# Feed-forward entry of a hybrid attention block: low parts and differences of two operand sets (H22, T4) made by VectorE instead of GpSimd

## The chip, the cores and the metric

The kernel runs on one core of a Trainium2 chip. A core has five engines, each with its own instruction queue: TensorE (matmul; PE in the profile, PEld its weight loads), VectorE (DVE), ScalarE (ACT), GpSimd (POOL) and SyncE (SP), which here only issues transfers. The metric is the device time of one execution in microseconds; the time of a kernel is the median over its runs.

## The reference

One transformer block over 1024 tokens of width 1024 in float32: a mixer (dilated attention and a gated delta rule side by side, with an output projection), then a gated feed-forward network of inner width 2816, then a last norm. What the change touches is the entry of the feed-forward network:

```python
h = _rmsnorm(x, norm_ffn_g[l]) * (1.0 + sc2) + sh2
y = (jax.nn.silu(h @ w_gate[l]) * (h @ w_up[l])) @ w_down[l]
x = x + g2 * y
return _rmsnorm(x, final_norm_g)
```

## The kernel before

Every large product is made in three matmuls: each float32 operand is split into a high part (a cast by ScalarE to the matmul's own format) and a low part (operand minus high part), and high by high, high by low and low by high are added up in PSUM. A low part is one subtraction of 128 x 512 elements, `h2_split` for the activations (line 1473) and `parts` for the weights (line 1580).

The products `h @ w_gate` and `h @ w_up` are made by a fast scheme that takes seven half-size products in place of eight. `h` is kept transposed as two halves of the width (four tiles of 128 each: k = 0 to 3 and 4 to 7) by two halves of the tokens (0 and 1). In `x2[d, hf]`, d is the tile of the width and hf the half of the tokens. The seven activation operands are H11 and H21 (the first half of the tokens), H22 (the second half's upper tiles), and T1 to T4, sums and differences of the quarters. Each operand consists of four tiles with a high and a low part: `H22h0`, `H22l0` and so on. The weights come as slabs of 128 x 512, 11 pairs f of gate (`wg`) and up (`wu`); their names in the profile are `wr` (as loaded), `wh` and `wl` (parts), `s` (sums).

`up_first` makes the two products that need only H11 and H21. The other five, in `rest_begin` and `up_rest`, follow one another on TensorE in the order T2, T1, T3, H22, T4, 12 matmuls each (`up_mm`, line 1590), into the PSUM banks a and c in turn. For the first three pairs f the products with H11 and H21 are made ahead (`early`), while the second half of the tokens is normed; then, from the line `t2 = []` on, VectorE and ScalarE make the five remaining operand sets:

- `normed2` (lines 1503 and 1506) norms a tile in place, VectorE and ScalarE after each other;
- T1 and T2 are differences of normed quarters (line 1596), split with low parts on VectorE;
- T3 likewise;
- H22 is the normed upper quarter itself: only a split;
- T4 is `x2[4 + k, 0] - t2[k]`, in place, then a split.

In the kernel before, the four low parts of H22, the four differences of T4 and the first two low parts of T4 are GpSimd's: ten operations. All high parts are ScalarE's.

The program is written as a list of operations with dependences; a scheduler puts each engine's operations in one fixed order, by priority and by its own estimate of when an operand is ready. Operations under `urgent()` (weight loads and parts, the sums between products) go ahead of others. So moving an operation to another engine changes the order on that engine, and of what depends on it on others. Each engine then takes its list strictly in order, waiting on semaphores.

Memory: the tiles `x2` and `t2` lie in the pool `px`, closed at `sx.close()`; the pool `po2` behind it takes the same room. It holds the raw slabs `wr2` of the second-half products, so the first of these loads wait until VectorE has read the last T3 operands.

Of the kernel before, what the change touches and what calls it, by code (L numbers as in the profile page):

```python
# [82 lines left out]
def build(tc, I, out):  # L83
    nc = tc.nc
# [442 lines left out]
    def scratch(name, n, shape):  # L527
        return [dr.tile(shape, F32, name=f"{name}{i}_d") for i in range(n)]

    class _:  # L530
# [12 lines left out]
        x2 = scratch("x2", 2, [4, P, D])  # L543
# [105 lines left out]
    t1, t2 = t12[:, 0:64], t12[:, 64:P]  # L649
# [810 lines left out]
    x2 = {}  # L1460
# [9 lines left out]
    def h2_split(name, k, src, lo_eng, copy=None):  # L1470
        hi, lo = HB[name][k]
        (copy or nc.scalar.copy)(hi, src)
        lo_eng.tensor_tensor(out=lo, in0=src, in1=hi.bitcast(F32), op=ALU.subtract)
# [121 lines left out]
    def sub(out, a, b, eng=None):  # L1595
        (eng or nc.vector).tensor_tensor(out=out, in0=a, in1=b, op=ALU.subtract)
# [133 lines left out]
    t2 = []  # L1730
# [13 lines left out]
        sub(x2[k, 1], x2[4 + k, 1], x2[k, 1])  # L1744
        h2_split("T3", k, x2[k, 1], nc.vector)
    for k in range(4):
        h2_split("H22", k, x2[4 + k, 1], nc.gpsimd)
    for k in range(4):
        sub(x2[4 + k, 0], x2[4 + k, 0], t2[k], nc.gpsimd)
        h2_split("T4", k, x2[4 + k, 0], nc.gpsimd if k < 2 else nc.vector)  # L1750
    sx.close()
    po2, so2 = pool("po2")
    for f in range(NF):
# [214 lines left out]
```

## Time and profile before

| | |
|---|---|
| median of 3 runs | 1414.42 us (1414.08, 1414.42, 1420.56) |
| the profiled execution | 1418.03 us, of it 1416.1 from the first to the last instruction |
| TensorE busy | 1354.1 us, 96% of the span |
| VectorE busy | 879.7 us, 62% |
| ScalarE busy | 661.3 us, 47% |
| GpSimd busy | 302.6 us, 21%, the last at 805.7 us |
| mean granted TensorE clock | 0.987 |

Times in the views count from the first instruction of the span. A busy share is a mean over stages; the stage of this change lies between 774 and 827 us. A row of a timeline gives the start, the duration, the engine, the line, the operation with the tiles that it writes and reads, and in brackets the time that the engine idled before it and what ended that. Rows of one line and form that follow each other are merged (x2).

### The profile page before, as it was taken

What the parts mean: (1) busy time and instruction counts of PE and PEld (TensorE: products, weight loads), DVE (VectorE), ACT (ScalarE), POOL (GpSimd) and SP (SyncE); (2) the same over time, 40 slices, a digit from 0 to 9 for tenths busy, and PEclk for the clock granted to TensorE, in tenths of its full rate; (3) what the DMA queues carried; (4) which work ended last, traced back from release to release, by engine and by line L of the source; (5) the groups of instructions that cost most, each with busy time, mean ns of one, the idle gap of its engine ahead of it and who ended that gap; (6) DMA issues with size and microseconds to landing.
All of it is one profiled execution on the core that took longest, in us unless ns stands there. A gap on an engine that the chain in (4) does not pass through costs nothing.

```text
span 1416.1 us, 24467 instructions
## 1 busy us (share of the span) xinstructions
PE 1354.1 (96%) x8984; PEld 1114.2 (79%) x8984; DVE 879.7 (62%) x1659; ACT 661.3 (47%) x1287; POOL 302.6 (21%) x277
## 2 busy tenths in 40 slices
PE   8998999999989899999999999999999999999997
PEld 5678877888888777768777778888888888888885
DVE  3688484655826433666228986757575776474487
ACT  4398424365234355766147633333333333444456
POOL 2345412443213344543252400000000000000000
PEclk9999999998999999999999999999999999999999
DMA  8656664485342345621584264545363565766566
GB/s 306 233 182 166 172 207 158 141 265 159 120 131 68 127 127 170 175 96 54 174 262 151 67 200 153 183 135 200 110 218 112 194 210 188 262 219 198 194 222 232
DMA packets 169872, 245.68 MB, mean 173 GB/s; under 512 B 32566, under 2 KB 73831, under 8 KB 169752
## 3 DMA queue, kind: packets, MB, share of 16 engines
q1 hardware_dynamic: 169752, 244.12, 53.3%
q8 instruction: 71, 1.16, 0.3%
q14 instruction: 49, 0.40, 0.1%
HBM read 181.30 MB, written 67.48 MB: 176 GB/s over the span
## 4 chain that ended last, share of the span: by engine, by line
PE 54%; DVE 5%; DMA 3%; issue 2%; ACT 1%; POOL 0%; SPq 0%; DVEq 0%; ACTq 0%; POOLq 0%
PE wua L1590 8%; PE wga L1590 8%; PE X L1785 6%; PE wuc L1590 4%; PE Z L1785 4%; PE wgc L1590 4%; PE wo L590 4%; PE g_a L590 3%; PE y L1348 2%; PE Y L1785 2%; PE tr L1331 2%; PE wgb L1590 2%; PE wub L1590 2%; PE S L1307 1%; PE S L1308 1%
## 5 line engine op out<-in xcount | busy, mean ns | idle before, releaser
L1580 DVE TENSOR_TENSOR wl_db<-wr_db,wh_db 128x512 fp32r<-128x512 f32 x77 | 53.2, 691 | 76.2 <-ACT wh_db L1579 76.0
L1579 ACT CAST wh_db<-wr_db 128x512 fp32r<-128x512 f32 x77 | 47.9, 622 | 98.0 <-PE X L1785 41.3
L1311 DVE CUSTOM_DVE_ANT_0 X<-S,ng 128x512 f32<-128x512 f32 (+3 forms) x64 | 36.8, 587 | 55.8 <-PE S L1308 38.0
L1785 PE MATMUL X<-wl_db,wh_da 128*128 128x512 f32 x176 | 68.6, 390 | 0.2 <-DVE wl_db L1580 0.2
L1785 PE MATMUL X<-wh_db,wl_da 128*128 128x512 f32 x176 | 68.5, 389 | 0.0
L1785 PE MATMUL X<-wh_db,wh_da 128*128 128x512 f32 x176 | 68.5, 389 | 0.0
L1316 ACT ACTIVATE X<-X,sc 128x128 f32<-128x128 f32 (+7 forms) x64 | 49.4, 773 | 38.5 <-DVE sc L1311 35.0
L1318 POOL TENSOR_SCALAR X<-X,sc 128x128 f32<-128x128 f32 (+7 forms) x64 | 50.5, 792 | 76.0 <-DVE sc L1317 72.6
L1580 DVE TENSOR_TENSOR wl_da<-wr_da,wh_da 128x512 fp32r<-128x512 f32 x77 | 52.7, 686 | 1.2 <-ACT wh_da L1579 1.2
L590 PE MATMUL g_a<-hh,wh_a 128*128 128x512 f32 x128 | 53.4, 417 | 0.0
L590 PE MATMUL wo<-yh,wh_wo 128*128 128x512 f32 x128 | 51.5, 405 | 0.9 <-DVE xo L1399 0.9
L590 PE MATMUL wo<-yl,wh_wo 128*128 128x512 f32 x128 | 50.4, 394 | 1.3 <-DVE yl L1410 1.3
L590 PE MATMUL g_a<-hh,wl_a 128*128 128x512 f32 x128 | 51.5, 402 | 0.0
L590 PE MATMUL g_a<-hl,wh_a 128*128 128x512 f32 x128 | 51.4, 402 | 0.0
L590 PE MATMUL wo<-yh,wl_wo 128*128 128x512 f32 x128 | 51.0, 398 | 0.0
L1579 ACT CAST wh_da<-wr_da 128x512 fp32r<-128x512 f32 x77 | 47.3, 616 | 5.9 <-PE wua L1590 5.8
L1331 PE MATMUL tr<-ident,X 128*128 128x128 f32 x288 | 44.0, 277 | 3.6 <-DVE et L1334 1.5
L1579 ACT CAST wh_wg_s<-wg_s 128x512 fp32r<-128x512 f32 x33 | 20.5, 621 | 55.1 <-PE wuc L1590 23.8
L231 POOL TENSOR_TENSOR wl_wo<-wr_wo,wh_wo 128x512 fp32r<-128x512 f32 x24 | 32.9, 1374 | 62.2 <-ACT wh_wo L230 62.2
L1331 PEld LDWEIGHTS tr<-ident,X 128*128 128x128 f32 x288 | 33.2, 140 | 13.3 <-issue 5.7
L613 PE MATMUL g_va<-wh_va,hh 128*128 128x256 f32 x128 | 38.3, 299 | 5.4 <-ACT sp_a L1096 5.4
L1348 PE MATMUL y<-et,va 128*64 128x128 f32 x576 | 43.2, 280 | 0.3 <-DVE yl L1360 0.3
(545 smaller groups left out, 4337.5 us busy)
## 6 DMA issues: line engine op xcount, KB each, us to landing
wm<-in_wada SPq DMA_DIRECT2D x44, 512.0 KB, 6.1
wr_da<-ao_d SPq DMA_DIRECT2D x77, 256.0 KB, 3.1
wr_wu<-in_wu SPq DMA_DIRECT2D x50, 256.0 KB, 2.7
wr_wg<-in_wg SPq DMA_DIRECT2D x48, 256.0 KB, 3.2
ao_d<-a SPq DMA_DIRECT2D x44, 256.0 KB, 2.4
wr_wd<-in_wdn SPq DMA_DIRECT2D x44, 256.0 KB, 3.1
wr_db<-wt_d SPq DMA_DIRECT2D x44, 256.0 KB, 2.7
ao_d<-as SPq DMA_DIRECT2D x33, 256.0 KB, 2.3
```

Source lines behind the costliest of these rows:

```text
L231: (eng or nc.gpsimd).tensor_tensor(out=lo[:, :n], in0=raw[:, :n], in1=hi[:, :n].bitcast(F32), op=ALU.subtract)
L590: last[0] = nc.tensor.matmul(ps, a[:, w0], b[k0 + k4][:, cs], start=(i == 0), stop=(i == n - 1))
L613: last[0] = nc.tensor.matmul(ps[:, :n], a[k][:, ts_], b[:, w0], start=(i == 0), stop=(i == 23))
L1311: nc.vector.tensor_tensor_reduce(out=X[:, c0:c1], in0=ps[:, 0 : c1 - c0], in1=ng[:, u + c0 : u + c1], scale=1.0, scalar=(3e38 if m is None ...
L1316: nc.scalar.activation(X[:, 0:nk], X[:, 0:nk], AF.Exp, scale=-1.0, bias=m, accum_out=sc[:, 2:3])
L1318: nc.gpsimd.tensor_scalar(out=X[:, 0:nk], in0=X[:, 0:nk], scalar1=sc[:, 3:4], scalar2=0.0, op0=ALU.mult, op1=ALU.add)
L1331: nc.tensor.transpose(ps[:, (kb - c0) * P : (kb - c0 + 1) * P], X[:, kb * P : kb * P + P], ident)
L1348: nc.tensor.matmul(yps[64 * e : 64 * e + 64, yc], va[:, kb, 64 * e : 64 * e + 64], ets[e][:, kb, :], start=(kb == 0), stop=(kb == qb),)
L1579: nc.scalar.copy(hi, src)
L1580: (eng or nc.vector).tensor_tensor(out=lo, in0=src, in1=hi.bitcast(F32), op=ALU.subtract)
L1590: nc.tensor.matmul(ps, a[:, w0], b, start=(first and k == 0 and n_ == 0), stop=(k == 3 and n_ == 2), skip_group_check=True,)
L1785: nc.tensor.matmul(bank[b], a[:, ts_], w, start=(first and f == 0 and n_ == 0), stop=(f == NF - 1 and n_ == 2), skip_group_check=True,)
```

## The change

The low parts of H22 and T4 and the differences of T4 are all given to VectorE.

```diff
@@ -1744,10 +1744,10 @@
     for k in range(4):
-        h2_split("H22", k, x2[4 + k, 1], nc.gpsimd)
+        h2_split("H22", k, x2[4 + k, 1], nc.vector)
     for k in range(4):
-        sub(x2[4 + k, 0], x2[4 + k, 0], t2[k], nc.gpsimd)
-        h2_split("T4", k, x2[4 + k, 0], nc.gpsimd if k < 2 else nc.vector)
+        sub(x2[4 + k, 0], x2[4 + k, 0], t2[k])
+        h2_split("T4", k, x2[4 + k, 0], nc.vector)
     sx.close()
```

The order of TensorE's operations and of SyncE's transfers stays as it is. On VectorE, at the end of the entry stage, between the last difference of T3 and the first product of gate and up (a11), rows come in (`x2_4_0` and its like are tiles of the first half of the tokens, names as in `x2[4, 0]`):

```order
 L1596 TENSOR_TENSOR x2_3_1_8146<-x2_7_1_8150,x2_3_1_8146 128x512
+L1473 TENSOR_TENSOR H22l0_8719<-x2_4_1_8147,H22h0_8718 128x512
+L1473 TENSOR_TENSOR H22l1_8721<-x2_5_1_8148,H22h1_8720 128x512
+L1473 TENSOR_TENSOR T3l3_8749<-x2_3_1_8146,T3h3_8748 128x512
+L1473 TENSOR_TENSOR H22l2_8723<-x2_6_1_8149,H22h2_8722 128x512
+L1473 TENSOR_TENSOR H22l3_8725<-x2_7_1_8150,H22h3_8724 128x512
+L1596 TENSOR_TENSOR x2_4_0_8151<-x2_4_0_8151,t2_0_9039 128x512
+L1596 TENSOR_TENSOR x2_5_0_8152<-x2_5_0_8152,t2_1_9048 128x512
+L1596 TENSOR_TENSOR x2_6_0_8153<-x2_6_0_8153,t2_2_9057 128x512
+L1473 TENSOR_TENSOR T4l0_8751<-x2_4_0_8151,T4h0_8750 128x512
```

All ten operations of GpSimd come in here, behind the differences of T3; nothing ahead of the T1 parts moves. The piece goes on, up to the sums of the first up-slab (`wu0_s1`):

```order
+L1599 TENSOR_TENSOR wg0_u5_9149<-wga0_8758,wg0_u5_9149 128x512
+L1473 TENSOR_TENSOR T4l1_8753<-x2_5_0_8152,T4h1_8752 128x512
 L1473 TENSOR_TENSOR T4l2_8755<-x2_6_0_8153,T4h2_8754 128x512
+L1596 TENSOR_TENSOR x2_7_0_8154<-x2_7_0_8154,t2_3_9066 128x512
+L1599 TENSOR_TENSOR wg0_u2_9148<-wgc0_9078,wg0_u2_9148 128x512
 L1473 TENSOR_TENSOR T4l3_8757<-x2_7_0_8154,T4h3_8756 128x512
-L1473 TENSOR_TENSOR T3l3_8749<-x2_3_1_8146,T3h3_8748 128x512
 L1684 TENSOR_TENSOR a11_0_9207<-p1_wg0_8772,p1_wu0_8838 128x512
 L1599 TENSOR_TENSOR wu0_s1_9221<-wr2_wu0_20_9217,wr2_wu0_21_9219 128x512
-L1599 TENSOR_TENSOR wg0_u5_9149<-wga0_8758,wg0_u5_9149 128x512
 L1596 TENSOR_TENSOR wu0_s2_9222<-wu0_s1_9221,wr_wu0_10_9213 128x512
```

The two sums of gate (`wg0_u5`, `wg0_u2`), which stood behind `wu0_s1`, now stand ahead of a11, among the T4 operations. On ScalarE the four high parts of T4 move from before the T3 parts to behind them:

```order
 L1472 CAST T3h3_8748<-x2_3_1_8146 128x512
 L1648 COPY wg0_u5_9149<-wgc0_9078 128x512
+L1472 CAST T4h0_8750<-x2_4_0_8151 128x512
+L1472 CAST T4h1_8752<-x2_5_0_8152 128x512
+L1472 CAST T4h2_8754<-x2_6_0_8153 128x512
 L1669 ACTIVATE wg0_u5_9149<-wg0_u5_9149 128x512
+L1472 CAST T4h3_8756<-x2_7_0_8154 128x512
+L1669 ACTIVATE wg0_u2_9148<-wg0_u2_9148 128x512
+L1669 ACTIVATE g21_0_9203<-wga0_8758 128x512
 L1579 CAST wh_wu0_s2_9227<-wu0_s2_9222 128x512
```

The two silu operations and g21 (line 1669), which stood among the parts of the up-slab, now stand ahead of its first high part.

## The prediction

> **What bounds the kernel now.** I looked first at the busy time by stretch (columns: stretch and length, then busy time and count of TensorE, its weight loads, VectorE, ScalarE and GpSimd, the granted clock, the DMA share, GB/s), cut where GpSimd does the ten operations that the diff moves.
>
> ```profile
> 774.00:802.20 28.20, 28.20 (x130) 23.44 (x129) 28.15 (x34) 22.10 (x40) 12.74 (x8) 1.00 0.36 112
> 802.20:827.05 24.85, 19.73 (x74) 14.27 (x74) 22.31 (x34) 10.69 (x20) 3.48 (x3) 0.93 0.36 118
> 827.05:1373.00 545.95, 545.95 (x2410) 452.09 (x2409) 360.96 (x566) 220.47 (x391) 0.00 (x0) 1.00 0.56 187
> ```
>
> Before 802.2 and from 827.05 to 1373 TensorE has no gap. Only the middle stretch can be shortened, and what is won there is kept, since TensorE alone sets the next 546 us. The timeline of TensorE shows the holes there (start, duration, operation, and in brackets the idle time and who ended it).
>
> ```profile
> 802.26 0.39 PE L1590 MATMUL wga<-T2h,wh_wg_s 128*128 128x512 f32 x1
> ...
> 806.89 0.50 PE L1590 MATMUL wga<-T2l,wh_wg_s 128*128 128x512 f32 x1 [2.20 <-DVE T2l L1473]
> ...
> 813.36 0.50 PE L1590 MATMUL wga<-T3h,wh_wg_s 128*128 128x512 f32 x1 [0.66 <-ACT wg_u L1646]
> ...
> 817.12 0.51 PE L1590 MATMUL wga<-T3l,wh_wg_s 128*128 128x512 f32 x1 [0.65 <-DVE T3l L1473]
> ...
> 824.65 0.50 PE L1590 MATMUL wua<-T2h,wl_wu_s 128*128 128x512 f32 x1 [0.88 <-DVE wl_wu_s L1580]
> ...
> 827.05 0.39 PE L1590 MATMUL wuc<-T1h,wh_wu_s 128*128 128x512 f32 x1
> ```
>
> Between the first and the last of these rows stand six blocks of 12 matmuls (wg with T2, T1, T3, H22, T4, then wu with T2). A block without a hole takes 2.72 us, as the chain of waits has it:
>
> ```profile
> 829.93 2.72 PE wua L1590 x12
> 832.65 2.72 PE wuc L1590 x12
> ```
>
> So 6 x 2.72 = 16.32 us of work took 827.05 - 802.26 = 24.79: **8.47 us are lost**, and that is the most that any change here can give. Most holes end on VectorE. VectorE itself never rests from 774 to 817, but its operations are not all of one length:
>
> ```profile
> 781.10 0.68 DVE L1599 TENSOR_TENSOR p_wu<-wub,p_wu 128x512 f32<-128x512 f32 x1
> 781.70 1.42 DVE L1580 TENSOR_TENSOR wl_wg<-wr_wg,wh_wg 128x512 fp32r<-128x512 f32 x1
> ...
> 792.47 1.79 DVE L1596 TENSOR_TENSOR wr_wg<-wr_wg,wr_wg 128x512 f32<-128x512 f32 x1
> 794.18 1.77 DVE L1473 TENSOR_TENSOR T2l<-t,T2h 128x512 fp32r<-128x512 f32 x1
> 795.88 1.77 DVE L1596 TENSOR_TENSOR x<-x,x 128x512 f32<-128x512 f32 x1
> ...
> 801.08 3.48 DVE L1473 TENSOR_TENSOR T1l<-x,T1h 128x512 fp32r<-128x512 f32 x2
> ...
> 806.15 0.68 DVE L1473 TENSOR_TENSOR T2l<-t,T2h 128x512 fp32r<-128x512 f32 x1
> ...
> 816.99 0.68 DVE L1684 TENSOR_TENSOR a<-p_wg,p_wu 128x512 f32<-128x512 f32 x1
> ```
>
> From 806.15 to 816.99 stand 18 operations: 10.84 / 18 = 0.602 us from start to start. From 781.70 to 816.99 stand 42, which at 0.602 would be 25.3 us and took 35.3: 10.0 us too much, all of it before 806.15 and in single operations that take 1.77 (0.68 elsewhere). Their places are those of GpSimd:
>
> ```profile
> 781.26 1.31 POOL L1596 TENSOR_TENSOR x<-x,t 128x512 f32<-128x512 f32 x1 [16.23 <-DVE t L1596]
> 786.20 3.38 POOL L1596 TENSOR_TENSOR x<-x,t 128x512 f32<-128x512 f32 x2 [3.63 <-DVE t L1596]
> 792.35 4.76 POOL L1473 TENSOR_TENSOR H22l<-x,H22h 128x512 fp32r<-128x512 f32 x3 [2.76 <-ACT H22h L1472]
> 798.90 1.70 POOL L1473 TENSOR_TENSOR H22l<-x,H22h 128x512 fp32r<-128x512 f32 x1 [1.80 <-ACT H22h L1472]
> 800.57 1.74 POOL L1596 TENSOR_TENSOR x<-x,t 128x512 f32<-128x512 f32 x1
> 802.28 3.41 POOL L1473 TENSOR_TENSOR T4l<-x,T4h 128x512 fp32r<-128x512 f32 x2
> ```
>
> Ten GpSimd operations, ten extra microseconds on VectorE: the two take turns, 1.70 us a pair (794.18, 795.88), about 1.1 of it GpSimd's.
>
> **The change part by part.** *Removed*: ten GpSimd operations, and with them the 10.0 us that VectorE stands behind them. *Added*: ten VectorE operations of the form in the rows above, 10 x 0.602 = 6.0 us, so VectorE as a whole is 4.0 us better off. But the order matters more than the sum: the ten stand behind the last T3 difference, so all before them (T2, T1, T3, the parts of wg's slabs) comes up to 10 us earlier, and only what follows pays the 6.0.
>
> I walk this along the new order, counting operations from the one at 781.70, at 0.602 each, plus 0.68 to the end, plus 0.4 for short waits on ScalarE: T2l0 is now reached at 782.30 and its high part is ready at 782.34 by the row below, a wait that did not show before; I allow a few of these. TensorE's demand is 802.26 plus 2.72 a block.
>
> ```profile
> 781.72 0.62 ACT L1472 CAST T2h<-t 128x512 fp32r<-128x512 f32 x1
> ```
>
> T2l3 (22 operations on): ready 796.0, wanted 804.5. T3l3 (41 on): 807.5, wanted 810.0. H22l3 (43 on): 808.7, wanted 812.7. T4l0 (47 on): 811.1, wanted 813.4. All in time, so the first holes close. T4l3 is later than its 53 places say: its high part waits for the last difference x_7_0 (51 on, ready 813.5) and ScalarE's 0.62, so it starts at 814.25 and is ready at 814.9, wanted at 815.4: 0.5 us of slack. Behind it on VectorE's queue stand a11, then the sums of the first up-slab, wu0_s1 (start 815.45) and wu0_s2, which needs wu0_s1's end (816.15 to 816.85). ScalarE's high part of wu0_s2 takes 0.62, so TensorE's wu block on T2 starts at 817.55 in place of 815.86: **1.7 us late**. Its third matmul needs the low part, three places after wu0_s2: 817.96 + 0.68 = 818.65, which costs **another 0.7**. That is the new wait; nothing else is late, and the next block starts at 818.58 + 2.4 = 820.98 in place of 827.05. Gain: 8.47 - 2.4 = **6.1 us**.
>
> What of the transfers? The up-slab's second pair of loads is released by VectorE's reads of T3l, and one of these loads is in the chain now:
>
> ```profile
> 816.46 0.61 DVE T3l L1473
> ...
> 817.09 0.33 SPq L1571
> ...
> 817.46 5.21 DMA wr_wg<-in_wg
> ...
> 822.70 0.69 DVE wg_s L1599
> ```
>
> These 5.2 us cost VectorE 2 us before wu0_s2's low part. With T3l3 ready at 807.5 even a 5.2 us load lands at 813, and its reader wg1_s1 comes at 817.4: covered by the ten inserted operations. Without that cover it would again cost 2.0. After 827 VectorE has slack: the low part of the next gate slab is made 8.6 us before its block.
>
> ```profile
> 829.33 0.68 DVE L1580 TENSOR_TENSOR wl_wg_s<-wg_s,wh_wg_s 128x512 fp32r<-128x512 f32 x1
> ...
> 837.93 0.39 PE L1590 MATMUL wga<-T2h,wh_wg_s 128*128 128x512 f32 x1
> ```
>
> In the new order it stands 67 places after 781.70 (822.8 with all waits named), wanted at 831.9: the same slack. GpSimd has no other work after this stage, so its idleness is free. ScalarE's casts of T4 move behind T3's; they are in the walk.
>
> The one price that no row gives exactly is that of the waits I put in by hand. Lower end: none (no 0.4, no wait before T4l3), then 1.4 us are lost instead of 2.4; upper end: each of the ten added operations waits 0.2 us on ScalarE (a third of its 0.62), 2 us more. I take 2.4, as the nearest rows (781.72) show waits under 0.4.
>
> The profiled execution took 1418.03 us (span 1416.1 and 1.9 around it): 1418.03 - 6.1 = 1411.9. It is 3.6 above the median of the runs, 1414.42; the stage is the same length in both as far as is known, so 1414.42 - 6.1 = **1408.3 us**.
>
> **A rule weighed.** TensorE's clock falls to half after the present hole:
>
> ```profile
> 805.47:808.88 3.41, 1.52 (x5) 0.97 (x6) 3.41 (x6) 0.81 (x2) 0.21 (x1) 1.00 0.00 0
> 808.88:812.29 3.41, 3.41 (x10) 2.62 (x8) 3.41 (x7) 2.64 (x6) 0.00 (x0) 0.50 0.23 77
> 733.79:737.20 3.41, 1.70 (x11) 1.15 (x9) 2.29 (x3) 2.28 (x5) 2.42 (x2) 1.00 0.97 267
> 737.20:740.61 3.41, 3.41 (x20) 2.82 (x19) 0.54 (x2) 1.10 (x2) 0.00 (x0) 1.00 1.04 305
> ```
>
> A window with 1.52 us of matmul was followed by 3.41 us at half clock, one with 1.70 was not. The new waits leave 3.41 - 2.4 = 1.0 us of matmul in the worst-placed 3.41 us, so a fall is possible: half of 3.41 is 1.7 us, 1410.0.
>
> The Trainium skill ("TensorE: Matmul & The Clock Gate", "What's actually happening") puts the fall after at least one idle window of about 3.4 us; by it the new waits cost no clock and the sum stays 1408.3. The trace differs: here a window that was 45% busy was enough.
>
> **The rivals.** (1) *The remaining wait is under 1.4 us*: my hand-put waits do not show and VectorE comes through at 0.60. For it: 18 operations in a row do so at 806 to 817. Against: wu0_s2 needs a chain of VectorE, ScalarE, TensorE that no order shortens. Gain 7.1 to 8.5, 1405.9 to 1407.3. (2) *The clock falls in the new gap*: 1410.0, decided by where the window lies. (3) *Only half of VectorE's slowness goes*, the rest being dependences: gain 2 to 3, about 1412. Against: the long operations stop with GpSimd's last one. (4) *Slower*: the slowness has nothing to do with GpSimd, and VectorE only gets ten operations more, at the ten places before wu0_s1: 6.0 us, 1420.4, or 1422.1 with a half-clock window; it decides if an operation beside no GpSimd work takes 1.77. Against: ScalarE rests for 3.86 us while VectorE is at its slowest, and the one operation that reads PSUM while GpSimd works (786.20 to 789.58) is not slow.
>
> ```profile
> 797.68 0.62 ACT L1472 CAST T1h<-x 128x512 fp32r<-128x512 f32 x1 [3.86 <-DVE x L1596]
> 788.36 0.68 DVE L1599 TENSOR_TENSOR p_wg<-wgb,p_wg 128x512 f32<-128x512 f32 x1
> ```
>
> The Trainium skill ("SBUF — State Buffer", "Who interferes with whom") has VectorE with two SBUF operands and GpSimd excluding each other for a whole instruction, and VectorE with one of them in PSUM not held; by it (4) is out. The trace agrees: 1.77 us for the one, 0.68 at 788.36 for the other.
>
> **How the numbers follow.** Forecast 43% (own range 1407.4 to 1409.4), (1) 40%, since the hand-put waits are as large as its distance, (2) 9%, (3) 4%, (4) 4%. What a measurement can tell from no change is about 0.5%, 7.07 us, and the forecast is 0.43%: faster takes (1), 0.40; slower most of (4), 0.03; the rest, 0.57, is within. Range: down to (1)'s end and a microsecond of scatter, 1405.0; up past (2) to (3), 1412.0.
>
> **What would show it.** Right: no VectorE operation over 0.75 us from 781 to 818; a11 near 814.9 instead of 816.99; no hole at T2, T3; one hole of 2 to 3 us at the first wu block on T2, ended by ScalarE's cast and VectorE's wl_wu_s; wuc's T1 near 821.0; the same 546 us after it. Wrong: 1.77 us operations without GpSimd, holes at T4l, a half-clock window near 819, or a gap after 827.

## The result and the profile after

| | before | changed |
|---|---|---|
| median of 19 runs each, taken together | 1415.45 us (1412.03 to 1421.39) | 1411.32 us (1407.40 to 1417.67) |
| ratio of the runs, 95% interval | | 0.9967 (0.9953 to 0.9980) |
| the profiled execution, its span | 1418.03, 1416.1 us | 1409.24, 1407.2 us |

The kernel is faster by 4.7 us by the ratio (0.0033 x 1415.45; 2.8 to 6.7 by its interval). The forecast, 6.1 us, lies inside this interval; its time, 1408.3 us, is 3.0 below the median.

The busy time by stretch of the changed kernel, at the marks used before (columns as there):

```profile
774.00:802.20 28.20, 28.20 (x127) 23.33 (x126) 28.20 (x47) 22.94 (x42) 0.00 (x0) 1.00 0.29 96
802.20:827.05 24.85, 23.18 (x101) 18.59 (x100) 24.61 (x41) 12.05 (x21) 0.00 (x0) 1.00 0.49 159
827.05:1373.00 545.95, 545.95 (x2410) 452.05 (x2410) 359.78 (x566) 221.75 (x392) 0.00 (x0) 1.00 0.56 188
```

GpSimd does nothing here any more. In the middle stretch TensorE does 101 matmuls where it did 74, at full clock throughout; some twelve of the 27 more are there only because this execution came to the stage 2.80 us earlier (see below). What follows is the same 545.95 us without a gap, so nothing won in the stage is given back. TensorE's timeline, with all the holes of the stage:

```profile
799.46 0.39 PE L1590 MATMUL wga<-T2h,wh_wg_s 128*128 128x512 f32 x1
...
814.46 0.50 PE L1590 MATMUL wua<-T2h,wh_wu_s 128*128 128x512 f32 x1 [1.24 <-ACT wh_wu_s L1579]
...
815.62 0.50 PE L1590 MATMUL wua<-T2h,wl_wu_s 128*128 128x512 f32 x1 [0.42 <-DVE wl_wu_s L1580]
...
818.02 0.39 PE L1590 MATMUL wuc<-T1h,wh_wu_s 128*128 128x512 f32 x1
...
828.90 0.39 PE L1590 MATMUL wga<-T2h,wh_wg_s 128*128 128x512 f32 x1
```

Between the same two matmuls as before lie 818.02 - 799.46 = 18.56 us in place of 24.79. Without holes they would be 16.32, so 2.24 us are lost in place of 8.47: **6.23 us are won in the stage**. The holes at T2 and T3 are gone; the two that are left end on ScalarE's high part and VectorE's low part of the first up-slab. VectorE's timeline:

```profile
778.90 0.68 DVE L1580 TENSOR_TENSOR wl_wg<-wr_wg,wh_wg 128x512 fp32r<-128x512 f32 x1
...
792.27 0.69 DVE L1473 TENSOR_TENSOR T2l<-t,T2h 128x512 fp32r<-128x512 f32 x1
...
803.70 0.68 DVE L1473 TENSOR_TENSOR T3l<-x,T3h 128x512 fp32r<-128x512 f32 x1
...
811.15 0.68 DVE L1473 TENSOR_TENSOR T4l<-x,T4h 128x512 fp32r<-128x512 f32 x1
811.75 0.68 DVE L1684 TENSOR_TENSOR a<-p_wg,p_wu 128x512 f32<-128x512 f32 x1
812.35 0.68 DVE L1599 TENSOR_TENSOR wu_s<-wr_wu,wr_wu 128x512 f32<-128x512 f32 x1
813.07 0.69 DVE L1596 TENSOR_TENSOR wu_s<-wu_s,wr_wu 128x512 f32<-128x512 f32 x1
...
814.88 1.28 DVE L1580 TENSOR_TENSOR wl_wu_s<-wu_s,wh_wu_s 128x512 fp32r<-128x512 f32 x2
```

From the first of these rows (the operation that stood at 781.70 before) to a11 at 811.75 are 54 operations in 32.85 us, 0.608 apart. Before they were 42 in 35.29 us. VectorE does twelve operations more (GpSimd's ten, and the two sums of gate that now stand ahead of a11) in 2.4 us less, and none of them takes over 0.75. The new order has one more difference that is not GpSimd's: the last low part of T2 and one part of a weight slab now stand ahead of two low parts of T1. That is two places, 1.2 us, for T2; it changes nothing in the count up to a11.

The profiled executions differ by more than the change explains: 8.9 us of span, of which 6.23 lie in the stage and 802.26 - 799.46 = 2.80 ahead of it. These 2.80 are there already at the first row above (778.90 against 781.70), before any of GpSimd's operations has held VectorE, and a second execution of the changed kernel came to the stage at 802.17. So the stage's own length, not the profiled total, measures the change.

### The profile page after: what moved, and what is told of

Read it like the earlier page. It is cut to its first block, busy times and chain, and to the rows that moved or that the text cites. A ratio compares the mean times of both kernels' runs of the same rounds, so it can differ in the third digit from the quotient of the medians.

```text
span 1407.2 us, 24465 instructions
## 1 busy us (share of the span) xinstructions
PE 1347.5 (96%) x8984; PEld 1109.5 (79%) x8984; DVE 875.2 (62%) x1669; ACT 661.7 (47%) x1287; POOL 285.8 (20%) x267
## 4 chain that ended last, share of the span: by engine, by line
PE 58%; DVE 3%; DMA 2%; issue 1%; ACT 1%; POOL 0%; SPq 0%; DVEq 0%; ACTq 0%; POOLq 0%
PE wua L1590 8%; PE wga L1590 8%; PE X L1785 6%; PE wo L590 5%; PE wgc L1590 4%; PE wuc L1590 4%; PE Z L1785 4%; PE g_a L590 3%; PE y L1348 3%; PE wgb L1590 2%; PE Y L1785 2%; PE wub L1590 2%; PE tr L1331 2%; PE S L1307 1%; PE S L1308 1%
```

## The experiments

Two of the experiments change TensorE's order inside the stage, so all kernels are compared over a longer stretch: from the first matmul of wg with T2 to the first of the next pair's wg with T2, ten blocks, 27.2 us without a hole (10 x 2.72). Each length comes from one execution; the two kernels that were profiled twice repeat it to 0.22 and 0.00 us. The medians are of 5 to 12 runs (19 for the first two rows), and each ratio is to runs of the kernel before made beside them. Those had medians of 1417.13 us for the kernels from "before again" to "four more on VectorE", 1417.97 for the two with g21 later and 1416.31 for the other four. So the medians of different groups are not to be compared with each other, but the ratios are.

| kernel | ten blocks, us | lost, us | median of its runs | ratio to before, interval |
|---|---|---|---|---|
| before | 35.67 | 8.47 | 1415.45 | |
| changed | 29.44 | 2.24 | 1411.32 | 0.9967 (0.9953 to 0.9980) |
| before again | 35.45 | 8.25 | 1418.28 | 1.0002 (0.9984 to 1.0021) |
| changed, GpSimd subtracts beside it | 41.74 | 14.54 | 1422.59 | 1.0033 (1.0009 to 1.0057) |
| changed, GpSimd fills beside it | 31.10 | 3.90 | 1410.37 | 0.9952 (0.9933 to 0.9972) |
| changed, four more on VectorE | 33.22 | 6.02 | 1415.49 | 0.9970 (0.9953 to 0.9988) |
| only H22 moved | 30.27 | 3.07 | 1413.93 | 0.9972 (0.9954 to 0.9990) |
| only T4 moved | 30.79 | 3.59 | 1411.46 | 0.9967 (0.9951 to 0.9983) |
| changed, a11 later | 29.01 | 1.81 | 1409.41 | 0.9943 (0.9924 to 0.9961) |
| changed, g21 later | 29.45 | 2.25 | 1412.14 | 0.9950 (0.9933 to 0.9967) |
| changed, a11 and g21 later | 28.85 | 1.65 | 1410.82 | 0.9944 (0.9923 to 0.9965) |
| changed again | 29.44 | 2.24 | 1411.59 | 0.9965 (0.9949 to 0.9981) |

The theory is the prediction's: a GpSimd operation that reads two tiles of SBUF holds back a VectorE operation that does the same. The rival is that VectorE's slowness in that stretch had another cause.

**The kernel before again**, unchanged, shows how far the stage repeats.

> The kernel before, once more, for how much its entry stage varies from one execution to the next. The stage is measured from the first matmul of wg's T2 block to the first of wuc's T1 block: 24.8 us in the profile of before, 18.6 in that of the changed kernel, 16.3 without a hole. If the stage's gain is the same in every execution, it is 24 to 25.5 us again, and the four to five microseconds that the runs show in place of six are scatter from elsewhere. Rival: the half-clock window in the stage of before was chance, and without it the stage is 1 to 2 us shorter, 23 to 24.

The stage took 24.56 us and the ten blocks 35.45, 0.22 under the first profile. 3.4 us of half clock fell in it again (806.59 to 810.00). It did not set the stage's length: the chain of waits of both profiles runs through VectorE's operations and then one load up to 824.19 (824.65 in the first), and the load explains the difference (4.96 us against 5.21). An execution of this kernel without half clock in the stage was not seen.

**GpSimd gets ten subtractions back, but nobody needs their results.** VectorE keeps all its operations; TensorE, VectorE and ScalarE have the same order as in the changed kernel.

```diff
         h2_split("T4", k, x2[4 + k, 0], nc.vector)
+    scr = pe.tile([P, HALF], F32R, name="scr", tag="eh", bufs=2)
+    for a, name in ((t2, "T2"), ([x2[4 + k, 1] for k in range(4)], "H22"), ([x2[k, 0] for k in range(2)], "T1")):
+        for k, s in enumerate(a):
+            nc.gpsimd.tensor_tensor(out=scr, in0=s, in1=HB[name][k][0].bitcast(F32), op=ALU.subtract)
     sx.close()
```

> The changed kernel with ten GpSimd subtractions of 128x512 added in the same stage, of the form of those taken away (operands T2, H22, T1 and their high parts), whose results nothing reads. Nothing waits for them and no other engine's order changes. Theory (GpSimd and VectorE take turns on two-operand work in SBUF, about 1.1 us each): VectorE's operations beside them take 1.7 to 1.8 again, a11 comes some 9 to 10 us later than in the changed kernel, the stage takes 26 to 29 us in place of 18.6, and the time is 7 to 10 us above the changed kernel, so 3 to 6 above the kernel before. Rival (VectorE was slow for its order and its waits on ScalarE, not for GpSimd): no operation over 0.75, stage 18.6, time as changed.

GpSimd's timeline in this kernel, and then VectorE's:

```profile
794.61 2.16 POOL L1754 TENSOR_TENSOR scr<-t,T2h 128x512 fp32r<-128x512 f32 x1 [6.76 <-ACT T2h L1472]
796.85 6.72 POOL L1754 TENSOR_TENSOR scr<-x,H22h 128x512 fp32r<-128x512 f32 x4
803.65 3.28 POOL L1754 TENSOR_TENSOR scr<-x,T1h 128x512 fp32r<-128x512 f32 x2
```

```profile
794.94 0.68 DVE L1473 TENSOR_TENSOR T2l<-t,T2h 128x512 fp32r<-128x512 f32 x1
795.54 1.77 DVE L1580 TENSOR_TENSOR wl_wg_s<-wg_s,wh_wg_s 128x512 fp32r<-128x512 f32 x1
797.24 3.47 DVE L1473 TENSOR_TENSOR T1l<-x,T1h 128x512 fp32r<-128x512 f32 x2
800.63 0.68 DVE L1599 TENSOR_TENSOR p_wg<-wgb,p_wg 128x512 f32<-128x512 f32 x1
...
804.04 3.44 DVE L1596 TENSOR_TENSOR x<-x,x 128x512 f32<-128x512 f32 x2
807.40 0.68 DVE L1580 TENSOR_TENSOR wl_wg_s<-wg_s,wh_wg_s 128x512 fp32r<-128x512 f32 x1
```

The 1.77 us operations are back beside GpSimd's work (whose first one waited itself, 2.16 us), and gone at 807.40, right behind its last one (803.65 + 3.28 = 806.93). At 795.54 the two engines work on different tiles, so it is not a tile that they share. The sum at 800.63, which has one operand in PSUM, takes 0.68 in the middle of it. a11 comes 22.01 us after the stage's start (821.41 - 799.40) in place of 12.29: 9.7 us for ten operations. The rival is out: GpSimd's work alone, with no dependence on it, makes the slowness. My expectation for the stage, 26 to 29 us, was too low (30.38 came): 18.56 + 9.72 = 28.28 would have been within, and the other 2.1 us go with 10.2 us at half clock behind the longer holes, which the expectation had left out.

**GpSimd writes only.** The same places in time, but the ten operations fill a tile and read no tile of 512 columns; a copy of one column ahead of each keeps them in place.

```diff
+    scr = pe.tile([P, HALF], F32R, name="scr", tag="eh", bufs=2).bitcast(F32)
+    for a in (t2, [x2[4 + k, 1] for k in range(4)], [x2[k, 0] for k in range(2)]):
+        for s in a:
+            nc.gpsimd.tensor_copy(scr[:, 0:1], s[:, 0:1])
+            nc.gpsimd.memset(scr, 0.0)
     sx.close()
```

> The changed kernel with ten GpSimd memsets of 128x512 added in the same stage, each behind a 128x1 copy that makes it wait for the same tiles; nothing reads their result. GpSimd is as busy in places, but reads only one column. If it is GpSimd's reading of SBUF that holds VectorE: stage 18.6 to 19.5 us, time as changed (within 1 us, apart from the ten small copies at 0.1 to 0.2 us of holding each). Rival (any GpSimd operation holds VectorE for its duration): operations of 1.2 us and more on VectorE, stage 22 us or more.

GpSimd's timeline, then VectorE's:

```profile
792.56 1.72 POOL L1754 COPY scr<-t 128x1 f32<-128x1 f32 x1 [6.55 <-DVE t L1596]
794.34 0.53 POOL L1755 MEMSET scr<- 128x512 f32 x1
794.93 0.55 POOL L1754 COPY scr<-x 128x1 f32<-128x1 f32 x1
795.54 0.53 POOL L1755 MEMSET scr<- 128x512 f32 x1
796.13 0.19 POOL L1754 COPY scr<-x 128x1 f32<-128x1 f32 x1
```

```profile
794.14 0.69 DVE L1580 TENSOR_TENSOR wl_wg_s<-wg_s,wh_wg_s 128x512 fp32r<-128x512 f32 x1
794.75 1.29 DVE L1473 TENSOR_TENSOR T1l<-x,T1h 128x512 fp32r<-128x512 f32 x2
795.95 0.69 DVE L1599 TENSOR_TENSOR p_wg<-wgb,p_wg 128x512 f32<-128x512 f32 x1
```

VectorE keeps its 0.60 us pitch beside the fills, and a11 again comes 12.29 us after the stage's start (813.02 - 800.73). A fill is shorter than a subtraction (0.53 us against 1.31), but VectorE was held for none of it, so the rival, that any GpSimd operation holds VectorE for its duration, is out: it is the reading that holds VectorE. Whether reading one tile in place of two would do is not tested. The Trainium skill ("SBUF — State Buffer", "Who interferes with whom") says that a VectorE instruction with two SBUF inputs contends with a GpSimd instruction that reads SBUF and not with one that only writes; this pair of runs agrees, 1.77 against 0.69 us.

The stage itself took 20.19 us, 1.6 more than the changed kernel's and 0.7 above the expected range. That is the clock, and the prediction's second rival. In these traces half clock begins and ends only on a grid of 3.413 us that holds for a whole execution. In the changed kernel's profile it stands from 117.47 to 120.88 and from 137.95 to 141.36, and 204 and 198 steps further on from their starts lies 813.79; in the kernel with fills it begins at 817.17. By these windows, first this kernel, then the changed one, each with the window that holds the second hole and the one behind it:

```profile
813.76:817.17 3.41, 1.69 (x7) 0.79 (x6) 3.32 (x6) 2.14 (x4) 0.00 (x0) 1.00 0.34 96
817.17:820.58 3.41, 3.41 (x9) 2.63 (x9) 3.41 (x7) 1.14 (x2) 0.00 (x0) 0.50 0.55 174
```

```profile
813.79:817.20 3.41, 2.31 (x9) 1.62 (x10) 3.41 (x6) 1.66 (x4) 0.00 (x0) 1.00 0.29 94
817.20:820.61 3.41, 3.41 (x17) 2.82 (x16) 3.41 (x7) 2.15 (x4) 0.00 (x0) 1.00 0.70 219
```

The holes are the same within 0.1 us. In the one kernel both lie in one window, 1.69 us of matmul are left in it, and the next window runs at half clock (0.50). In the other the edge at 813.79 cuts the first hole (813.22 to 814.46), 2.31 us are left, and the clock stays up. The window begins 13.03 us after the stage's start in the one and 14.33 in the other, and that is not in the program: it differs between executions.

**Four more operations on VectorE**, which nobody needs, among the H22 and T4 parts; all other orders are those of the changed kernel.

```diff
+    scr = pe.tile([P, HALF], F32R, name="scr", tag="eh", bufs=2)
+    for k in range(4):
+        nc.vector.tensor_tensor(out=scr, in0=x2[4 + k, 1], in1=HB["H22"][k][0].bitcast(F32), op=ALU.subtract)
     sx.close()
```

> The changed kernel with four more VectorE subtractions of 128x512 whose results nothing reads, placed among those of H22; no other order changes. Theory (what is left of the loss is VectorE's queue ahead of the first up-slab's sums, 0.60 an operation): wu0_s2 comes 2.4 us later, the stage takes 20.8 to 21.0 us in place of 18.6, the time is 2.4 above the changed kernel. Rival (the remaining hole is set by the loads or by ScalarE): less than 1 us more.

TensorE's timeline at the first block of wu with T2:

```profile
820.09 0.50 PE L1590 MATMUL wua<-T2h,wh_wu_s 128*128 128x512 f32 x1 [3.68 <-ACT wh_wu_s L1579]
...
821.25 0.79 PE L1590 MATMUL wua<-T2h,wl_wu_s 128*128 128x512 f32 x1 [0.43 <-DVE wl_wu_s L1580]
```

The hole grew from 1.24 to 3.68, 2.44 us or 0.61 for each operation: what is added to VectorE's queue ahead of the first up-slab lengthens the hole one for one. The stage took 22.32 us (824.98 - 802.66), 1.3 above the expected range, which had left the clock out: the rest of the 3.78 us by which the ten blocks grew goes with 3.4 us at half clock behind this hole. The expected 2.4 us in the time of the runs are not shown, the ratios are alike (0.9970 and 0.9967).

**Only H22 moved**: T4's differences and two of its low parts go back to GpSimd, six operations.

```diff
-        sub(x2[4 + k, 0], x2[4 + k, 0], t2[k])
-        h2_split("T4", k, x2[4 + k, 0], nc.vector)
+        sub(x2[4 + k, 0], x2[4 + k, 0], t2[k], nc.gpsimd)
+        h2_split("T4", k, x2[4 + k, 0], nc.gpsimd if k < 2 else nc.vector)
```

> H22's four low parts stay on VectorE as in the changed kernel; T4's four differences and two of its low parts go back to GpSimd (six of the ten operations). Theory (a GpSimd subtraction that reads two tiles holds a two-tile VectorE operation back by about 1.1 us, against the 0.60 VectorE needs to do it itself): each operation given back costs VectorE 1.1 - 0.6 = 0.5 us, 3 us for six if all lie beside VectorE work; some of them lie beside operations that read PSUM or beside waits, so the stage from wg with T2 to wuc with T1 takes 19.2 to 21.5 us (18.56 in the changed kernel, 24.79 before), with VectorE operations over 1.2 us only where GpSimd works. Rival (the loss before came from H22's low parts alone, which GpSimd did beside T2 and T1; T4's come later and spare VectorE six operations): 16.3 to 17.5 us. A half-clock window behind the hole adds up to 1.7 us to either.

In this kernel and the next TensorE begins wu with T1 before wu with T2 is done, so the end of the six blocks means nothing; over ten blocks (four more, 10.88 us) the theory's range is 30.1 to 32.4 us and the rival's 27.2 to 28.4. 30.27 us came. GpSimd's timeline, then VectorE's:

```profile
785.97 3.40 POOL L1596 TENSOR_TENSOR x<-x,t 128x512 f32<-128x512 f32 x2 [3.64 <-DVE t L1596]
796.02 4.68 POOL L1596 TENSOR_TENSOR x<-x,t 128x512 f32<-128x512 f32 x1 [6.65 <-DVE t L1596]
800.66 2.55 POOL L1473 TENSOR_TENSOR T4l<-x,T4h 128x512 fp32r<-128x512 f32 x2
```

```profile
796.46 1.28 DVE L1473 TENSOR_TENSOR T1l<-x,T1h 128x512 fp32r<-128x512 f32 x2
...
799.47 0.68 DVE L1599 TENSOR_TENSOR p_wg<-wgb,p_wg 128x512 f32<-128x512 f32 x1
801.91 1.85 DVE L1580 TENSOR_TENSOR wl_wg_s<-wr_wg,wh_wg_s 128x512 fp32r<-128x512 f32 x1 [1.76 <-ACT wh_wg_s L1579]
```

Only four VectorE operations are long here, 3.4 us in all for six GpSimd operations. One of these was itself the loser (796.02, 4.68 us), and others fell beside a rest of VectorE. So the six cost VectorE about what it saved by not doing them (6 x 0.60 = 3.6; a11 comes 12.47 us after the stage's start, against 12.29 in the changed kernel). But they cost it early, ahead of T3, where TensorE then waits 0.84, 0.28 and 0.65 us, and the saving comes later, ahead of wu. The ten blocks lie in the theory's range, although its net price on VectorE, 0.5 us an operation, was too high.

**Only T4 moved**: H22's four low parts go back.

```diff
-        h2_split("H22", k, x2[4 + k, 1], nc.vector)
+        h2_split("H22", k, x2[4 + k, 1], nc.gpsimd)
```

> The other part: only H22's four low parts go back to GpSimd, all of T4 is VectorE's. Theory: four times 1.1 - 0.6 = 2 us at most, stage 19.0 to 20.6 us, long VectorE operations beside T2 and T1 as before. Rival (T4's operations on GpSimd made the loss): 16.3 to 17.0 us, since VectorE has four operations (2.4 us) fewer ahead of the first up-slab. Taken with the other part: if both parts cost something, the change is worth its whole only with all ten operations off GpSimd. A half-clock window behind the hole adds up to 1.7 us.

Over ten blocks the theory says 29.9 to 31.5 us, the rival 27.2 to 27.9; 30.79 came. GpSimd's timeline, then VectorE's beside it:

```profile
789.25 7.37 POOL L1473 TENSOR_TENSOR H22l<-x,H22h 128x512 fp32r<-128x512 f32 x4 [27.32 <-ACT H22h L1472]
```

```profile
790.87 1.19 DVE L1580 TENSOR_TENSOR wl_wg_s<-wg_s,wh_wg_s 128x512 fp32r<-128x512 f32 x1
791.99 1.78 DVE L1596 TENSOR_TENSOR t<-x,x 128x512 f32<-128x512 f32 x1
793.69 1.78 DVE L1596 TENSOR_TENSOR wg_s<-wr_wg,wg_s 128x512 f32<-128x512 f32 x1
795.39 1.78 DVE L1473 TENSOR_TENSOR T1l<-x,T1h 128x512 fp32r<-128x512 f32 x1
797.09 0.68 DVE L1473 TENSOR_TENSOR T2l<-t,T2h 128x512 fp32r<-128x512 f32 x1
```

Three times 1.09 and once 0.5 are 3.8 us, against 4 x 0.60 = 2.4 saved. Neither part alone makes the loss: taking either group off GpSimd wins most of it (5.40 and 4.88 us of 6.23), the other then adds 0.83 or 1.35. The ratios of these two and of the changed kernel are not to be told apart; only the stage tells, from one execution of each.

**a11 later**: the changed kernel, with the first product of gate and up, and its store, behind the low part of the first up-slab (`held` keeps that instruction). The silu g21 is written behind it too, but on ScalarE it keeps its place right ahead of the slab's high part. The edit adds two lines ahead of these, so the line numbers in the views are higher by two.

```diff
-        nc.vector.tensor_tensor(out=a11, in0=g11, in1=c11, op=ALU.mult)
-        keep(0, f, a11)
+        if f:
+            nc.vector.tensor_tensor(out=a11, in0=g11, in1=c11, op=ALU.mult)
+            keep(0, f, a11)
...
+        if not f:
+            with tc.issue_after(held["wu0_s2"].ins):
+                silu(g21, gbank)
+                nc.vector.tensor_tensor(out=a11, in0=g11, in1=c11, op=ALU.mult)
+                keep(0, f, a11)
```

> The changed kernel, with only the first product of gate and up (a11 of f = 0, and its store) put on VectorE behind the low part of the first up-slab; the order of the other engines' operations stays. Theory (the hole that is left is VectorE's queue up to the sum of that slab): the hole at the first wu block on T2 shrinks by one operation, 0.6 us, stage 17.9 to 18.1 us. Rival (the hole is set by the load of the slab or by ScalarE's casts, not by the number of VectorE operations): 18.56 us as in the changed kernel. The median of the runs should then lie 0 to 1 us below the changed kernel's in the same call, which is near what the runs can tell.

TensorE's only hole in the ten blocks:

```profile
816.77 0.50 PE L1592 MATMUL wua<-T2h,wh_wu_s 128*128 128x512 f32 x1 [1.24 <-ACT wh_wu_s L1581]
```

The stage took 18.13 us (819.90 - 801.77), 0.43 less than the changed kernel's, between the two expectations and nearer to the theory's. But the first hole stayed at 1.24; what went is the second. The theory had missed a second bound, which ScalarE's timeline of the changed kernel shows:

```profile
813.31 0.60 ACT L1669 ACTIVATE g<-wga 128x512 f32<-128x512 f32 x1 [1.41 <-PE wga L1590]
813.80 1.13 ACT L1579 CAST wh_wu_s<-wu_s 128x512 fp32r<-128x512 f32 x2
```

g21, which waits for TensorE's T4 block, stands ahead of the slab's high part and lets it start at 813.80, just when VectorE's sum is ready too (813.07 + 0.69 = 813.76). Two queues end within 0.04 us of each other, and shortening one wins nothing at that hole. Two more kernels test this.

**g21 later, alone and with a11.** On ScalarE, g21 goes behind the slab's high part (here `held` keeps the cast); the second kernel has a11 moved as well.

```diff
-        silu(g21, bank)
+        if f:
+            silu(g21, bank)
+        gbank = bank
...
         u12, u22, bank = up_rest(f, "wu", au, ru)
+        if not f:
+            with tc.issue_after(held["wu0_s2"].ins):
+                silu(g21, gbank)
```

> The changed kernel, with one operation of ScalarE moved: the silu g21, which waits for the end of the T4 block and stands ahead of the high part of the first up-slab, goes behind it; the order of the other engines stays. In the changed kernel g21 leaves ScalarE free 14.34 us after the start of the stage, and VectorE's sum of the slab is ready at 14.30: two bounds at once. Theory (VectorE's queue binds as well): nothing is won, stage 18.4 to 18.6 us. Rival (the hole of 1.24 us is ScalarE's alone, by g21): the high part starts 0.5 us earlier, stage 17.9 to 18.1 us.

> Both moved behind the first up-slab's parts: a11 on VectorE and g21 on ScalarE. Theory (both queues bound the first hole together): the high part is ready at 14.4 in place of 15.0 us after the start of the stage, and the hole of 1.24 us falls to 0.6 to 0.7; the low part, which VectorE makes two operations after the sum, becomes the next bound (ready at about 15.5), so that a second hole of 0.4 to 0.7 us opens and the stage takes 17.7 to 18.0 us against 18.13 with a11 alone. Rival (neither queue sets the first hole, but the end of the T4 block itself): 1.24 us stay and the stage takes 18.1 us.

The stages took 18.57 us (818.80 - 800.23) and 17.97 (820.93 - 802.96), within the theory's range in both. TensorE's timeline of the kernel with both moved:

```profile
817.42 0.50 PE L1592 MATMUL wua<-T2h,wh_wu_s 128*128 128x512 f32 x1 [0.70 <-ACT wh_wu_s L1581]
...
818.53 0.50 PE L1592 MATMUL wua<-T2h,wl_wu_s 128*128 128x512 f32 x1 [0.37 <-DVE wl_wu_s L1582]
```

Only with both queues shortened does the first hole fall, from 1.24 to 0.70; the low part's 0.37 is then next. In the ten blocks this kernel beats the kernel before by 6.82 us and the changed one by 0.59. By the runs it and the one with a11 alone (0.9944 and 0.9943) are faster than the kernel before, as the changed kernel is; that they beat the changed kernel too is not shown by the runs, whose intervals overlap with 0.9965 (0.9949 to 0.9981).

**The changed kernel again.**

> The changed kernel once more, unchanged, beside the others. Median 1410 to 1412 us, ratio 0.9953 to 0.998. Its stage takes 18.5 to 18.7 us if the clock stays up behind the hole, 19.9 to 20.3 if a half-clock window of 3.4 us falls there; if the latter is seen, the runs' smaller gain (4.1 to 4.7 us against 6.2 in the stage) is partly this.

Median 1411.59 us, ten blocks 29.44 us to the hundredth, no half clock behind the hole. The first case of the expectation.

## Why the prediction was right, point by point

- *8.47 us are lost and can be won, nothing after 827 changes that*: right; the next 545.95 us are the same without a gap.
- *GpSimd's ten operations cost VectorE 10.0 us*: right, and shown both ways. Taken away, 54 operations run at 0.608; put back without any dependence, a11 is 9.7 us later; as writes only, they cost nothing.
- *T2, T1, T3, H22, T4 come in time*: right. T4l3 was ready at 811.83, 12.37 us after the stage's start, where the walk had 12.64 (814.9 - 802.26); TensorE waits for no part of T4. (The walk's own sum for T4l3's start is a little off: 813.5 + 0.62 is 814.1, not 814.25.)
- *A new wait at the first up-slab, 1.7 for the high part and 0.7 for the low, 2.4 in all*: right in place and in what ends the holes, a little too large. The block started at 814.46, 1.40 after the 813.06 of five blocks without a hole, and ended 0.84 over its 2.72: 2.24. a11 came 12.29 us after the stage's start, 0.3 before the walk's 12.59: of the 0.64 us of waits put in by hand (0.4, and 0.24 ahead of T4l3) 0.34 came, the time by which the 54 operations took longer than 54 x 0.602. The cause was only one of two: the walk put it all down to VectorE's queue and left out g21, the silu ahead of the high part on ScalarE; both bind at the same moment (four more operations on VectorE add 0.61 us each, one fewer takes nothing off the first hole, both queues shortened take 0.54).
- *The loads are covered*: no wait of TensorE or VectorE in the stage ends on a load; the cover was not taken away, so its price stays untested.
- *Gain 6.1*: 6.23 in the stage, in both profiles of the changed kernel.
- *1408.3 us in all*: 3.0 too low. 1.0 of it is the base: 1414.42 was the median of three runs, and 19 gave 1415.45. The other 2.0 is the gain, 4.1 by the medians. The interval of the ratio holds 6.1, so the runs don't say that anything is missing. What could be missing is rival (2): half clock in the new gap costs 1.66 us in the kernel with fills (31.10 - 29.44) and was absorbed in the old one, where VectorE was the bound. Neither of the changed kernel's two profiles has it; of the four executions that have both holes at nearly these sizes (these two, the fills, g21 later) one has. How often it falls there is open, since the runs' times alone do not show where the clock fell. By the median alone rival (2), 1410.0, and rival (3), 1412, stand nearer than the forecast; it is the rows of the stage that decide for its mechanism.
- *Rival (1)*, under 1.4 us lost: not so, 2.24. Its bound was out of the walk's reach from the start: without the 0.64 us put in by hand, 2.4 becomes 1.76 and not 1.4. So its chance of 40% rested on a bound that the walk does not give. *Rivals (3) and (4)*: out, by the two runs with GpSimd beside the changed kernel.

## What to carry to other kernels

An operation given to an idle engine is not free when the two engines stand in each other's way: here a GpSimd subtraction on two SBUF tiles cost VectorE 0.6 to 1.1 us, and VectorE does the same in 0.60. To see it, look on the busy engine for operations of one form with two durations (0.68 and 1.77), and on the other engine for what runs beside the long ones. Then price the move by the order of the queue, not by the sum: what the moved operations now stand ahead of, and who waits for that.

## What the runs showed of the hardware

- Who loses is not fixed. Mostly the two took turns, 1.70 us a pair. But with only H22 moved, a GpSimd difference took 4.68 us (1.29 at its first one) while VectorE ran five operations at 0.60 beside it, until VectorE's sum from PSUM. With GpSimd filling, it was mostly the one-column copies that waited, 0.3 to 1.72 us in place of 0.18.
- A window of 3.41 us need not be idle for the clock to halve. 1.52 (the kernel before) and 1.69 us of matmul in it (the fills) were followed by half clock, 1.70 (the kernel before, at 733.79) and 2.31 (the changed kernel) were not. The busy time alone does not give the border: in the changed kernel the window from 134.54 to 137.95 held 2.81 us of smaller matmuls (most of them 64*128) and was followed by half clock. The Trainium skill ("TensorE: Matmul & The Clock Gate", "What's actually happening") puts the fall after at least one idle window; here windows that were about half busy and more were followed by it.
